# Issue order in the MLP of a decoder step: the second unit's first block, the last activations of a quarter, a third weight sum and the last unit's weight split are issued at other places

## The chip, the cores and the metric

The kernel runs on one NeuronCore of one Trainium2 chip. The metric is the time on the device in microseconds, the median of several runs. Engines: TensorE (PE), VectorE (DVE), ScalarE (ACT), GpSimd (POOL) and SyncE (SP), whose queue issues all the DMAs here.

## The reference, cut to what matters

One layer of a hybrid decoder for 512 prompt tokens and 64 sample tokens (8 requests of 8), width 1024. Attention, a gated recurrence and the first layer norm come first; the change lies in the MLP and the second layer norm behind it:

```python
x1 = _layer_norm(DN_ALPHA * x + g1 * mix, ln1_g, ln1_b, dtype)
u2 = x1 * (1 + sc2) + sh2
hid = jnp.square(jax.nn.relu(jnp.einsum('bsd,df->bsf', u2, w_up) + b_up))
ff = jnp.einsum('bsf,fd->bsd', hid, w_down) + b_down
x2 = _layer_norm(DN_ALPHA * x1 + g2 * ff, ln2_g, ln2_b, dtype)
```

`w_up` is 1024 x 4096, `w_down` 4096 x 1024, all in float32. To keep float32 accuracy at the matmul's fast format, every operand is split in a high part and a low part (the operand minus its high part), and a product is three matmuls: high by high, low of the data by high weight, high of the data by low weight.

## The kernel before, in words

**Weights.** A *unit* is a block of 1024 x 512 weights (eight k of 128 rows), loaded in two DMAs of 1 MB into `wraw` tiles; there are three such tiles (`NRAW`). `weights_done` frees one after its last reading and issues the next load. A weight block is split by an ACT copy to `whi` (the *cast*) and a subtraction to `wlo` (*low*), mostly on DVE. `split_k` (L362) does that for one k (128 x 512) into two tiles of the common pool `pages` (62 of them); the MLP's steps put theirs into the pool `parts` (6 tiles of 128 x 1024), which opens at L2092 in the memory that `front.close()` gives back.

**Order.** The order on each engine is the order in which the program issues; nothing is reordered afterwards, and an instruction whose input isn't there holds all behind it on its engine. A planner (`Engine`, `Side`) keeps a modelled clock of each engine, and between matmuls `side.pump` issues pieces of side work (layer norm, transposes, stores) whose modelled inputs are ready.

**The MLP.** `hid` is made and used in four quarters of 1024 columns. Tokens are handled in two halves of 288 columns (`HF`).

- *First unit of quarter 0* (L1796 to L1809): the first token half of its four blocks runs while the first layer norm's second half is still under way (`layer_norm_1(1)`, which makes the operands `U2_hi`, `U2_lo` tile by tile). Then `side.drain()`, then the second half of all four blocks, k by k into four PSUM banks (two of tag "lin", two of tag "att"), then `ups[n]`: for each bank ACT does relu, square and the high copy `hdh`, DVE the low part `hdl`.
- *The rest* is a list `seq` of 70 steps, run by the loop at L2101. `Plain` steps (L1884) are one block of 128 output columns over eight k, in two token halves (`pe(0)`, `pe(1)`, each 24 matmuls); they are the second unit of quarter 0 (steps 0 to 3) and the down-projections of quarters 0 to 2 (8 each). `Seventh` steps (L1944) are the seven products of Strassen's scheme for the up-projections of quarters 1 to 3: two units a quarter, seven steps f0 to f6 each, 24 matmuls a step. f1, f2, f4 and f5 need a sum of two weight blocks first (`sum`, on DVE, into `wraw`).
- In the loop, at step i, the order is: evacuation of step i-1's second half; cast of step i+1 if its `lag` is 1 (a Plain); low of step i+1; cast of step i+2 if its lag is over 2; if step i is a Plain right behind a Seventh: low part of step i-2's output (`sub`), activation of step i-1's (`fin`), its low part (`sub`); then `pe(0)` and its evacuation; on Sevenths the `fin` of i-1 and `sub` of i-2; the sum for step i+3 if its lag is over 2; sum and cast of step i+2 if its lag is 2; then `pe(1)`. f1 and f2 have lag 2, the other Sevenths lag 3.
- The first down-projection of quarters 1 and 2 uses `order`: second token half first, k in the order 0, 1, 2, 3, 6, 7, 4, 5, as k=4, 5 of that half (f5) and k=6, 7 of the first half (f6) come last.

**The end** (L2147 to L2283): the last quarter's down-projection in three units `ud[0]`, `ud[1]`, `ud[2]`. `blocks` makes output columns with the tokens 256 to 575 as the moving side, four blocks n a unit; behind each comes `gated` (DVE) and `tokens_major` (transposes, copies by ACT and DVE). `tiles` makes the tokens 0 to 255 as rows, two tiles c of 128 by 512 columns; `add_up` takes them into the residual on DVE, `moments` and `normalize` end a tile, DVE and POOL sharing the columns. The order is `blocks(ud[0])`, `blocks(ud[1])`, `tiles(ud[1])`, `tiles(ud[2])`. `ud[1]` is split in the last block of `blocks(ud[0])` (`pass_on`); `ud[2]` is split inside `tiles(ud[1])` at every second k: k 0 to 3 in tile 0 with the subtraction on POOL, k 4 to 7 in tile 1 with the subtraction on DVE. The side work normalises the tiles c = 2, 3, 4 in that same stretch.

Of the kernel before, what the change touches and what calls it, by code (L numbers as in the profile page):

```python
# [19 lines left out]
KT = D // 128  # L20
# [31 lines left out]
NPG = 62  # L52
NKV = 6
NWP = 6
AHEAD_K = 8
LN2 = 2500
SPH = 0
NRAW = 3
KV_AHEAD = 4
QB_AHEAD = 4  # L60
# [185 lines left out]
def decoder_step(ctx, tc, I, O):  # L246
# [24 lines left out]
    def bank(shape, tag, bufs=2):  # L271
        return psum.tile(shape, F32, name=tag, tag=tag, bufs=bufs)
# [86 lines left out]
        if j == len(u["blocks"]) - 1:  # L359
            weights_done(u["slots"])  # L360

    def split_k(u, k, eng=V):  # L362

        if k in u["w"]:
            return
        load_more(True)
        t = u["slots"][k // 4][2][:, k % 4]
        w = u["w"][k] = page([128, 512], "whi", F32R), page([128, 512], "wlo", F32R)
        A.activation(w[0], t, AF.Copy)
        eng.tensor_sub(w[1], t, w[0])  # L370
        if k % 4 == 3:
            weights_done(u["slots"][k // 4:k // 4 + 1])

# [1421 lines left out]

    u = mlp[0]  # L1796
    ups = [up_evac(0, n, True) for n in range(4)]
    for n in range(4):
        for m in range(n + 1, min(n + 3, 4)):
            split_once(u, m)  # L1800
        half(u, n, U2, 0, ups[n])
    side.drain()
    banks = [bank([128, HF], "lin" if n < 2 else "att") for n in range(4)]
    for k in range(KT):
        for n in range(4):
            mm_part(u["w"][n], 8, U2, 1, banks[n], (k,))
    for n in range(4):
        ups[n](1, banks[n])
        u["w"].pop(n)  # L1809

    def down_evac(qd, n):
        def evac(hf, ps):
            if qd == 0:
# [130 lines left out]
    class Seventh(Step):  # L1944


        def __init__(self, unit, f):
            self.U, self.f = unit, f
            self.lag = 2 if f in (1, 2) else 3

        def sum(self):
            f, b = self.f, self.U.blk
# [86 lines left out]
    for qd in range(4):  # L2039
        for n in range(8):  # L2040
            if qd == 0 and n < 4:
                continue
            if qd == 0:
                seq.append(Plain(mlp[1], n % 4, U2, up_evac(0, n)))
            elif n % 4 == 0:
                unit_ = Unit(mlp[qd * 4 + n // 4], qd, n)
                seq += [Seventh(unit_, f) for f in range(7)]
        if qd < 3:
            for n in range(8):

                order = {} if qd == 0 or n else {"order": ((1, (0, 1, 2, 3, 6, 7, 4, 5)), (0, range(KT)))}
                seq.append(Plain(mlp[qd * 4 + 2 + n // 4], n % 4, (Hd[0], Hd[1]), down_evac(qd, n), **order))
# [35 lines left out]
                yield 436, None  # L2088
        gate.append(True)

    front.close()
    parts["pool"] = ctx.enter_context(tc.tile_pool(name="parts", bufs=NWP))  # L2092
    n_down = len(seq) - 22

    def at(i, what, *a):
        if 0 <= i < len(seq):
            getattr(seq[i], what)(*a)

    at(0, "cast")
    at(0, "low")  # L2100
    for i, st in enumerate(seq):  # L2101
        if i < 4:
            for k in (2 * i, 2 * i + 1):
                for h in range(2):
                    G.tensor_mul(hv(hT[k], h), hv(hT[k], h), rstds[h])
        if i == 4:
            side.add("p", input_sums())
        if i == 12:
            side.drain()
        if n_down <= i < n_down + 8:  # L2110
            if i == n_down:
                side.flush(True)
                reload(0)
            if i < n_down + 7:
                reload(i - n_down + 1)
        at(i - 1, "ev", 1)
        if i + 1 < len(seq) and seq[i + 1].lag == 1:
            at(i + 1, "cast")
        at(i + 1, "low")
        if i + 2 < len(seq) and seq[i + 2].lag > 2:  # L2120
            at(i + 2, "cast")
        if i and isinstance(st, Plain) and isinstance(seq[i - 1], Seventh):
            for n in (1, 2):
                at(i - n, "fin" if n == 1 else "sub")
            at(i - 1, "sub")
        st.pe(0)
        st.ev(0)
        if not isinstance(st, Plain):
            at(i - 1, "fin")
            at(i - 2, "sub")  # L2130
        if i + 3 < len(seq) and seq[i + 3].lag > 2:
            at(i + 3, "sum")
        if i + 2 < len(seq) and seq[i + 2].lag == 2:
            at(i + 2, "sum")
            at(i + 2, "cast")

        for k in {5: (0, 1), 4: (2, 3), 2: (4, 5), 1: (6, 7)}.get(len(seq) - i, ()):
            split_k(ud[0], k)
        if i >= 6 and i % 2 == 0:
            copy_rows()  # L2140
        st.pe(1)
# [90 lines left out]
    def blocks(w, e):  # L2232
        for n in range(4):
            ps = bank([128, NT - NM], "lin")
            for k in range(KT):
                if n == 0 and k + AHEAD_K < KT:
                    split_k(w, k + AHEAD_K)
                for m, (xi, wi) in enumerate(TERMS):
                    PE.matmul(ps, w["w"][k][wi][:, n * 128:(n + 1) * 128], HD[xi][k][:, NM:NT],
                              start=(k == 0 and m == 0), stop=(k == KT - 1 and m == 2))  # L2240
# [5 lines left out]
            side.add("pr"[n % 2], tokens_major(4 * e + n))  # L2246
            side.pump(6 * 136.0)

    def pass_on(u, k, v):

        if k >= 2:
            u["w"].pop(k - 2)
        if k >= KT - AHEAD_K:
            split_k(v, k - KT + AHEAD_K)

    def tiles(w, e):
        for c in range(NM // 128):
            last = c == NM // 128 - 1

            def before(k):  # L2260
                if w is ud[1]:
                    if last and k >= 2:
                        w["w"].pop(k - 2)
                    if k % 2 == SPH:
                        split_k(ud[2], 4 * c + k // 2, V if c else G)

            for cols in (slice(0, 256), slice(256, 512)) if e and last else (slice(0, 512),):
                ps = mm_tokens(w["w"], HD, lambda t: t[:, c * 128:c * 128 + 128], range(KT), before, cols,
# [51 lines left out]
```

## Time and profile before

| | |
|---|---|
| median of 3 runs | 1382.89 us (1377.75 to 1384.52) |
| the profiled execution | 1378.02 us, its span 1376.2 us |
| mean granted TensorE clock | 0.989 |
| MLP and end | from 947 us (the first unit's first half) to the end |
| Strassen stretches | 1059 to 1105, 1160 to 1203, 1255 to 1300 us |
| `tiles` of the end | from 1336.8 us |

In timeline rows the columns are start, duration, engine, line, operation, output<-inputs, shape and count; in brackets the idle time of the engine before it and what ended it. All instructions carry L175, the line of the helper that issues them, so tiles tell them apart. Rows with a count (x4) are several instructions merged.

### The profile page before, as it was taken

To read this page: it belongs to the slowest core of one execution; us is meant where nothing else is said; L and a number is where in the kernel's file an instruction comes from. 1 tells how busy PE (TensorE), PEld (TensorE's weight loads), DVE (VectorE), ACT (ScalarE), POOL (GpSimd) and SP (SyncE) were. 2 spreads that over 40 slices of the span, in tenths; PEclk is the share of its full clock that TensorE was granted. 3 is DMA by queue.
4 is the path that set the end of the run, shared out by engine and by line. 5 is a ranking of instruction groups with operands and counts; after the bars stand their busy time and mean duration, and the time that the engine had idled before them with its cause. 6 is when DMAs were issued, how large, how long until landed. Compare 5 with 4: busy or idle time off the path is not lost.

```text
span 1376.2 us, 24394 instructions
## 1 busy us (share of the span) xinstructions
PE 1315.5 (96%) x9480; PEld 1209.6 (88%) x9480; DVE 840.3 (61%) x1674; ACT 519.9 (38%) x1161; POOL 324.7 (24%) x371
## 2 busy tenths in 40 slices
PE   6999999999999999999999999999899999999995
PEld 3889898899878887888989999998899999999994
DVE  2457556558767886666655436547455744756858
ACT  2423333332332222332232442325455732744732
POOL 1232023027417573234343300002410000000005
PEclk9999999999999999999999999999999999999998
DMA  9789899789988977776454313331054433544512
GB/s 306 246 309 323 270 299 355 242 273 324 281 290 286 317 252 242 231 252 200 138 167 141 100 62 123 130 123 62 0 177 153 169 138 117 206 161 154 215 61 69
DMA packets 186824, 274.11 MB, mean 199 GB/s; under 512 B 16012, under 2 KB 92628, under 8 KB 186196
## 3 DMA queue, kind: packets, MB, share of 16 engines
q1 hardware_dynamic: 186708, 272.54, 58.7%
q8 instruction: 75, 1.23, 0.4%
q14 instruction: 41, 0.34, 0.1%
HBM read 212.81 MB, written 76.46 MB: 210 GB/s over the span
## 4 chain that ended last, share of the span: by engine, by line
PE 76%; DVE 10%; DMA 5%; ACT 4%; issue 3%; POOL 1%; SPq 1%; DVEq 0%; POOLq 0%; ACTq 0%
PE lin L175 58%; PE att L175 9%; PE sx L175 6%; DVE wlo L175 4%; PE tr L175 3%; DMA wada<-in_w_ada_dram 2%; DVE res L175 1%; ACT whi L175 1%; ACT sn L175 1%; DMA qb<-qsc 1%; SPq L175 1%; ACT hdh L175 1%; DMA out_dram<-kv 1%; DVE Op L175 1%; DVE hf L175 1%
## 5 line engine op out<-in xcount | busy, mean ns | idle before, releaser
L175 DVE TENSOR_TENSOR wlo<-wraw,whi 128x512 fp32r<-128x512 f32 (+1 forms) x334 | 271.1, 849 | 122.9 <-ACT whi L175 120.0
L175 PE MATMUL lin<-uh,whi 128*128 128x288 f32 x992 | 298.7, 301 | 5.1 <-DVE hso L175 2.4
L175 PE MATMUL lin<-ul,whi 128*128 128x288 f32 x992 | 299.5, 302 | 1.2 <-DVE ul L175 1.2
L175 PE MATMUL lin<-uh,wlo 128*128 128x288 f32 x992 | 298.6, 301 | 1.9 <-DVE wlo L175 1.9
L175 ACT ACTIVATE whi<-wraw 128x512 fp32r<-128x512 f32 (+1 forms) x338 | 211.6, 676 | 118.6 <-PE lin L175 37.0
L175 PEld LDWEIGHTS lin<-ul,whi 128*128 128x128 f32 x992 | 188.0, 189 | 13.8 <-issue 11.0
L175 PEld LDWEIGHTS lin<-uh,whi 128*128 128x128 f32 x992 | 187.8, 189 | 11.3 <-issue 2.9
L175 PEld LDWEIGHTS lin<-uh,wlo 128*128 128x128 f32 x992 | 188.1, 190 | 6.6 <-issue 3.8
L175 POOL TENSOR_TENSOR qb<-qb,kv 128x512 f32<-128x512 f32 x96 | 128.5, 1355 | 203.5 <-PE att L175 65.1
L175 PE MATMUL lin<-hdl,whi 128*128 128x288 f32 (+1 forms) x448 | 133.5, 298 | 4.0 <-DVE hdl L175 4.0
L175 PE MATMUL lin<-hdh,whi 128*128 128x288 f32 (+1 forms) x448 | 134.1, 299 | 0.0
L175 PE MATMUL lin<-hdh,wlo 128*128 128x288 f32 (+1 forms) x448 | 133.2, 297 | 0.0
L175 PEld LDWEIGHTS lin<-hdl,whi 128*128 128x128 f32 x448 | 84.5, 189 | 4.7 <-DVE hdl L175 4.7
L175 POOL TENSOR_TENSOR wlo<-wraw,whi 128x512 fp32r<-128x512 f32 x4 | 6.4, 1603 | 331.5 <-ACT whi L175 331.5
L175 PEld LDWEIGHTS lin<-hdh,whi 128*128 128x128 f32 x448 | 84.5, 189 | 0.0
L175 PEld LDWEIGHTS lin<-hdh,wlo 128*128 128x128 f32 x448 | 84.4, 188 | 0.0
L175 PE MATMUL lin<-whi,uh 128*128 128x512 f32 x160 | 68.4, 428 | 1.3 <-ACT whi L175 1.1
L175 PE MATMUL lin<-wlo,uh 128*128 128x512 f32 x160 | 63.9, 400 | 1.9 <-DVE wlo L175 1.9
L175 DVE TENSOR_REDUCE sc<-qb 128x4 f32<-128x512 f32 x96 | 63.7, 678 | 2.6 <-POOL qb L175 2.4
L175 PE MATMUL lin<-whi,ul 128*128 128x512 f32 x160 | 63.1, 394 | 0.0
L175 PE MATMUL lin<-u2h,whi 128*128 128x288 f32 x176 | 53.0, 301 | 6.1 <-ACT whi L175 4.9
L175 POOL TENSOR_TENSOR hk<-hk,T 128x256 f32<-128x256 f32 (+1 forms) x48 | 40.2, 838 | 72.0 <-PE att L175 43.4
(421 smaller groups left out, 2884.5 us busy)
## 6 DMA issues: line engine op xcount, KB each, us to landing
wraw<-in_w_in_dram SPq DMA_DIRECT2D x42, 1024.0 KB
kv<-in_cache_kv_w_dram SPq DMA_DIRECT2D x144, 256.0 KB
qb<-qsc SPq DMA_DIRECT2D x96, 256.0 KB
wraw<-in_w_down_dram SPq DMA_DIRECT2D x18, 1024.0 KB
out_dram<-kv SPq DMA_DIRECT2D x64, 256.0 KB
wraw<-in_w_ada_dram SPq DMA_DIRECT2D x16, 1024.0 KB
wraw<-in_w_up_dram SPq DMA_DIRECT2D x16, 1024.0 KB
out_dram<-in_cache_kv_w_dram SPq DMA_DIRECT2D x32, 512.0 KB
```

What stands on the lines that cost most here:

```text
L175: return f(out, *args, **kw)
```

## The change

1. The second token half of the first unit is issued later in the program, behind `front.close()`, the opening of `parts` and cast and low of step 0, which so stand ahead of it.
2. In the first unit of each quarter (`n == 0`) f2 gets lag 3: its sum is issued one step earlier, and its cast at the beginning of step f0, ahead of that step's matmuls. The block for lag 2 is put ahead of the sum for lag 3, so that f1's sum still precedes f2's.
3. At a Plain behind a Seventh, `sub`, `fin`, `sub` of the two steps before are issued ahead of cast and low of the next step.
4. `ud[2]` is no longer split in `tiles(ud[1])`. In `blocks(ud[1])`, at k = 2 of block n, two k at a time are split by one ACT and one DVE instruction of 128 x 1024 into the `parts` pool (n = 0, 1, 2), and k = 6, 7 by `split_k` into pages (n = 3). POOL no longer subtracts weights. `AHEAD_K` was 8, which equals the number of k, so that taking it out changes nothing.

```diff
@@ split_k
-    def split_k(u, k, eng=V):
+    def split_k(u, k):
...
-        eng.tensor_sub(w[1], t, w[0])
+        V.tensor_sub(w[1], t, w[0])
@@ first unit (moved, see below)
-    for n in range(4):
-        for m in range(n + 1, min(n + 3, 4)):
-            split_once(u, m)
-        half(u, n, U2, 0, ups[n])
-    side.drain()
-    banks = [bank([128, HF], "lin" if n < 2 else "att") for n in range(4)]
-    for k in range(KT):
-        for n in range(4):
-            mm_part(u["w"][n], 8, U2, 1, banks[n], (k,))
-    for n in range(4):
-        ups[n](1, banks[n])
-        u["w"].pop(n)
@@ class Seventh
-        def __init__(self, unit, f):
+        def __init__(self, unit, f, after):
             self.U, self.f = unit, f
-            self.lag = 2 if f in (1, 2) else 3
+            self.lag = 2 if f == 1 or f == 2 and not after else 3
...
-                seq += [Seventh(unit_, f) for f in range(7)]
+                seq += [Seventh(unit_, f, n == 0) for f in range(7)]
@@ ahead of the loop
-    front.close()
-    parts["pool"] = ctx.enter_context(tc.tile_pool(name="parts", bufs=NWP))
...
+    for n in range(4):
+        for m in range(n + 1, min(n + 3, 4)):
+            split_once(u, m)
+        half(u, n, U2, 0, ups[n])
+    side.drain()
+    front.close()
+    parts["pool"] = ctx.enter_context(tc.tile_pool(name="parts", bufs=NWP))
     at(0, "cast")
     at(0, "low")
+    banks = [bank([128, HF], "lin" if n < 2 else "att") for n in range(4)]
+    for k in range(KT):
+        for n in range(4):
+            mm_part(u["w"][n], 8, U2, 1, banks[n], (k,))
+    for n in range(4):
+        ups[n](1, banks[n])
+        u["w"].pop(n)
@@ the loop
         at(i - 1, "ev", 1)
+        if i and isinstance(st, Plain) and isinstance(seq[i - 1], Seventh):
+            at(i - 2, "sub")
+            at(i - 1, "fin")
+            at(i - 1, "sub")
         if i + 1 < len(seq) and seq[i + 1].lag == 1:
             at(i + 1, "cast")
         at(i + 1, "low")
         if i + 2 < len(seq) and seq[i + 2].lag > 2:
             at(i + 2, "cast")
-        if i and isinstance(st, Plain) and isinstance(seq[i - 1], Seventh):
-            for n in (1, 2):
-                at(i - n, "fin" if n == 1 else "sub")
-            at(i - 1, "sub")
         st.pe(0)
         st.ev(0)
         if not isinstance(st, Plain):
             at(i - 1, "fin")
             at(i - 2, "sub")
-        if i + 3 < len(seq) and seq[i + 3].lag > 2:
-            at(i + 3, "sum")
         if i + 2 < len(seq) and seq[i + 2].lag == 2:
             at(i + 2, "sum")
             at(i + 2, "cast")
+        if i + 3 < len(seq) and seq[i + 3].lag > 2:
+            at(i + 3, "sum")
@@ blocks
-                if n == 0 and k + AHEAD_K < KT:
-                    split_k(w, k + AHEAD_K)
+                if w is ud[1] and k == 2:
+                    if n < 3:
+                        split_two(ud[2], 2 * n)
+                    else:
+                        split_k(ud[2], 6)
+                        split_k(ud[2], 7)
@@ new
+    def split_two(u, k):
+        load_more(True)
+        t = u["slots"][k // 4][2][:, k % 4:k % 4 + 2]
+        hi, lo = (wpart([128, 2, 512], nm) for nm in ("whi", "wlo"))
+        A.activation(hi, t, AF.Copy)
+        V.tensor_sub(lo, t, hi)
+        for i in range(2):
+            u["w"][k + i] = hi[:, i], lo[:, i]
+        if k % 4 == 2:
+            weights_done(u["slots"][k // 4:k // 4 + 1])
@@ tiles
             def before(k):
-                if w is ud[1]:
-                    if last and k >= 2:
-                        w["w"].pop(k - 2)
-                    if k % 2 == SPH:
-                        split_k(ud[2], 4 * c + k // 2, V if c else G)
+                if w is ud[1] and last and k >= 2:
+                    w["w"].pop(k - 2)
```

More of the change, by code (lines that the diff above doesn't have):

```diff
@@ L54 @@
 NWP = 6
-AHEAD_K = 8
 LN2 = 2500
-SPH = 0
 NRAW = 3
@@ L2252, in pass_on @@
             u["w"].pop(k - 2)
-        if k >= KT - AHEAD_K:
-            split_k(v, k - KT + AHEAD_K)
+        split_k(v, k)
     def tiles(w, e):
```

## Prediction

> **What bounds the kernel now.** I read the page first, then the waits of PE, then the timeline engine by engine at each of those waits.
>
> ```profile
> PE 1315.5 (96%) x9480; PEld 1209.6 (88%) x9480; DVE 840.3 (61%) x1674; ACT 519.9 (38%) x1161; POOL 324.7 (24%) x371
> ...
> ```
>
> ```profile
> PE lin L175 <- DVE wlo L175: 8.9, 9, 3.0
> PE lin L175 <- ACT whi L175: 6.0, 2, 4.9
> PE lin L175 <- DVE hdl L175: 4.0, 3, 1.6
> ...
> ```
>
> PE is busy for 96% of the span, so 60.7 us of idle PE is all that reordering can take out (slow matmuls aside). The change issues the same arithmetic in another order; it touches three of the sources: the split weights (`whi`, `wlo`) and the low part of the activations (`hdl`). What counts is therefore each wait by itself, and at the very end, where PE has run dry, the engine that sets the end.
>
> **Part 1, the second unit's first block.** The timelines of PE, of ACT (first row the last `u2h` of the layer norm), of DVE and of POOL around 975 us:
>
> ```profile
> 975.58 0.29 PE L175 MATMUL att<-u2h,wlo 128*128 128x288 f32 x1
> 980.75 0.40 PE L175 MATMUL lin<-u2h,whi 128*128 128x288 f32 x1 [4.88 <-ACT whi L175]
> 984.66 0.29 PE L175 MATMUL lin<-u2h,whi 128*128 128x288 f32 x1
> ```
>
> and, from the windows view of PE (stretch, length, busy time, count, granted clock, share and rate of the DMAs),
>
> ```profile
> 985.00:1060.00 75.00, 75.00 (x568) 1.00 0.42 151
> ```
>
> ```profile
> 969.80 1.10 ACT L175 ACTIVATE u2h<-u2t,b2m 128x288 fp32r<-128x288 f32 x2 [0.39 <-DVE u2t L175]
> ...
> 974.71 0.50 ACT L175 ACTIVATE rel<-lin,vT 128x288 f32<-128x288 f32 x1 [3.80 <-PE lin L175]
> ...
> 979.73 0.44 ACT L175 ACTIVATE hdh<-rel 128x288 fp32r<-128x288 f32 x1
> 980.08 2.18 ACT L175 ACTIVATE whi<-wraw 128x512 fp32r<-128x512 f32 x4
> 986.06 0.50 ACT L175 ACTIVATE rel<-lin,vT 128x288 f32<-128x288 f32 x1 [3.80 <-PE lin L175]
> ...
> 992.64 0.49 ACT L175 ACTIVATE rel<-lin,vT 128x288 f32<-128x288 f32 x1
> ...
> 999.39 0.48 ACT L175 ACTIVATE rel<-lin,vT 128x288 f32<-128x288 f32 x1
> ```
>
> ```profile
> 970.37 1.08 DVE L175 SCALAR_TENSOR_TENSOR u2l<-u2t,b2m,u2h 128x288 fp32r<-128x288 f32 x2
> ...
> 980.73 2.50 DVE L175 TENSOR_TENSOR wlo<-wraw,whi 128x512 fp32r<-128x512 f32 x4
> ```
>
> ```profile
> 987.26 3.33 POOL L175 TENSOR_TENSOR hT<-hT,lnr 128x288 f32<-128x288 f32 x4
> ```
>
> The columns are start, duration, engine, line, operation and tiles. The unit's second half ends with the matmul at 975.58, and the next starts at 980.75: ACT does twelve evacuation instructions from 974.71 to 980.2 first, and only then the cast that step 0 waits for. PE's pace undisturbed is 75.00 / 568 = 0.132 us a matmul, so 5.17 - 0.13 = 5.0 us are lost. Behind the wait PE is slow: from 980.75 to 984.66 there are 15 matmuls, 3.91 us where 15 x 0.132 = 1.98 would do, 1.9 us more (part 4 has the clock in such a stretch). The stall costs 6.9 us.
>
> With the cast ahead of the evacuations it runs behind the last `u2h`, from 970.9, and its subtraction behind the last `u2l`, from 971.5; a block's cast and low are half of the four merged instructions each, 1.1 and 1.3 us, so both are ready by 973 while PE works to 975.8. What they wait for is the load of that unit:
>
> ```profile
> GB/s 0 186 406 254 0 0 179 397 263 0 7 0 0 0 0 10 0 0 0 0 3 104 387 341 14 0 0 0 0 0 0 0 0 7 0 0 0 0 0 0
> ```
>
> These are 40 slices of 2.5 us from 900 us on; the weight traffic is over at 962.5, ahead of 970.9. What is late next is the bank: step 0 reuses the first "lin" bank, which ACT has read at 974.71 + 0.50 = 975.2, ahead of 975.7. So the 6.9 us go. Then step 1's cast stands behind the evacuations as before, to 981.2, and the read of step 0's first bank behind that, to 981.7; PE wants that bank at 975.7 + 48 x 0.132 = 982.0. From there ACT, which waits for POOL's square, which stands behind four products for the layer norm (the 3.33 us), gives a bank back every 992.64 - 986.06 = 6.6 and 999.39 - 992.64 = 6.75 us, where PE takes a step in 6.34. Before, the 5 us wait had given that chain a lead. Now the lead is 0.3 us and is gone after a step; two steps at 0.4 us each, so 0.8 us come back. Bounds: 0 and 1.6 (four steps at 0.4). **Gain 6.1 us** (5.3 to 6.9).
>
> **Part 2, the third sum.** DVE and the chain in the first unit of quarter 1, and PE in its second:
>
> ```profile
> 1062.33 1.22 DVE L175 TENSOR_TENSOR wlo<-wraw,whi 128x1024 fp32r<-128x1024 f32 x1 [2.40 <-ACT whi L175]
> ```
>
> ```profile
> 1065.57 3.20 PE sx L175 x24
> ```
>
> ```profile
> 1089.02 0.40 PE L175 MATMUL att<-t23h,wlo 128*128 128x288 f32 x1 [0.73 <-DVE wlo L175]
> ```
>
> f2's low part is ready at 1062.33 + 1.22 = 1063.5 and f2 starts at 1065.57: two microseconds to spare, and no wait of PE in that unit. The wait of 0.73 us for `wlo` is at f2 of the *second* unit of the quarter, whose lag stays 2. So this edit moves a DVE sum of 1.2 us (as long as a subtraction of that size) and a cast to an earlier place and takes no wait away. The DVE sum now stands behind f1's sum, which is the one that can wait for a load; it adds no wait of its own. **0 us**; bounds three times 1.2 us on either side, if an evacuation of the down-projection gets stuck behind it or f2 of the second unit profits; I see neither in the queue, and take 0.
>
> **Part 3, the last activations.** PE, ACT and DVE where quarter 1's down-projection begins, and PE in quarter 2:
>
> ```profile
> 1107.13 0.29 PE L175 MATMUL lin<-hdh,whi 128*128 128x288 f32 x1
> 1108.63 0.40 PE L175 MATMUL lin<-hdl,whi 128*128 128x288 f32 x1 [1.20 <-DVE hdl L175]
> ...
> 1206.74 0.40 PE L175 MATMUL lin<-hdl,whi 128*128 128x288 f32 x1 [1.21 <-DVE hdl L175]
> ```
>
> ```profile
> 1105.19 0.78 ACT L175 ACTIVATE hdh<-sn 128x288 fp32r<-128x288 f32 x2
> ```
>
> ```profile
> 1106.91 1.29 DVE L175 TENSOR_TENSOR wlo<-wraw,whi 128x512 fp32r<-128x512 f32 x2 [2.73 <-ACT whi L175]
> 1108.12 1.56 DVE L175 TENSOR_TENSOR hdl<-sn,hdh 128x288 fp32r<-128x288 f32 x4
> ```
>
> f5's high part is there at 1105.19 + 0.78 = 1106.0, but its low part is the first of the four merged instructions at 1108.12, because the next block's split stands ahead of it in DVE's queue and that waits for its cast. PE stands until 1108.63: 1.50 - 0.13 = 1.4 us, and the same in quarter 2 (1.21 of idle against 1.20). Issued first, the subtraction takes f5's part at 1106.0 and is done by 1106.8, ahead of 1107.26. f6's part is needed 42 matmuls (5.5 us) after the block begins, and the next block's cast, now behind `fin`, comes about 1 us later with a lead of a step. The third `hdl` wait of the list, 4.0 - 1.20 - 1.21 = 1.6 us, is that behind the loop's end, whose order stays. **Gain 2.8 us** (2.4 to 3.0).
>
> **Part 4, the last unit's weights.** PE's waits from 1310 us to the end, its clock behind the longest, its last matmul, and DVE's queue:
>
> ```profile
> PE lin L175 <- DVE wlo L175: 4.3, 3, 3.0
> ```
>
> ```profile
> 1360.10:1363.30 3.20, 3.20 (x16) 0.50 0.17 36
> ```
>
> ```profile
> 1366.58 0.28 PE L175 MATMUL att<-wlo,hdh 128*128 128x256 f32 x1
> ```
>
> ```profile
> 1322.87 0.48 DVE L175 SCALAR_TENSOR_TENSOR hT<-lin,mod,hT 128x256 f32<-128x256 f32 x1
> ...
> 1346.96 1.00 DVE L175 TENSOR_TENSOR wlo<-wraw,whi 128x512 fp32r<-128x512 f32 x1
> 1347.88 3.48 DVE L175 SCALAR_TENSOR_TENSOR res<-res,lnst,lgb 128x512 f32<-128x512 f32 x2
> 1351.29 3.46 DVE L175 TENSOR_TENSOR wlo<-wraw,whi 128x512 fp32r<-128x512 f32 x2
> 1354.67 3.43 DVE L175 SCALAR_TENSOR_TENSOR res<-res,lnst,lgb 64x512 f32<-64x512 f32 x2
> 1358.03 0.68 DVE L175 TENSOR_TENSOR wlo<-wraw,whi 128x512 fp32r<-128x512 f32 x1
> 1358.63 0.67 DVE L175 TENSOR_TENSOR gps<-lin,gate 128x512 f32<-128x512 f32 x1
> ...
> 1363.85 1.53 DVE L175 SCALAR_TENSOR_TENSOR res<-res,lnst,lgb 128x512 f32<-128x512 f32 x2
> ```
>
> ```profile
> 1326.10 0.55 PE L175 MATMUL tr<-ident,hT 128*128 128x128 f32 x3 [0.48 <-ACT res L175]
> ```
>
> PE loses 4.3 us here, and half of 3.2 us at a granted clock of 0.50. But the end is DVE's: from 1346.96 on, each row begins where the one before it ends, and the `gps` of a tile that PE has long finished comes at 1358.63. So the gain is what leaves DVE's queue. Between 1346.96 and 1358.63 four subtractions of weights stand between the normalisations; without them the next tile's `gps` starts after the two pairs, 1346.96 + 3.48 + 3.43 = 1353.9, which is 4.8 us earlier. A pair costs 1.53 us at 1363.85 and 3.4 where POOL works on its own share of the normalisation at the same time. Were all pairs at 1.53, DVE would be faster still, and PE would set the end: last matmul 1366.58 - 4.3 - 1.6 = 1360.7, 5.9 us earlier. I take 5.0, near the lower end, since POOL's share of the normalisations stays and only its four weight subtractions go. The Trainium skill (SBUF - State Buffer, section on SBUF's two separate sides) says that a DVE instruction with two SBUF inputs and a GpSimd instruction exclude each other, one being blocked for the other's whole length; by that rule the pairs stay slow and the gain is the 4.8, by the quick row it is the 5.9. The trace is on the rule's side, 3.4 against 1.53.
>
> What it costs in `blocks(ud[1])`: three DVE instructions of 128 x 1024 (1.22 us as the `wlo` at 1062.33) and two of 128 x 512 (0.68). DVE is late there as it is: the last gating of `ud[0]` starts at 1322.87, behind the splits of `ud[1]`, and PE has 0.48 us of wait at 1326.10 for a copy that hangs on this. The first wide subtraction lands in this backlog, so that this wait grows by up to 1.2 us; the later ones come where DVE has caught up. I take 1.2 (0 to 5, if every one is passed on to PE). **Gain 3.8 us** (0 to 5.9).
>
> **Sum.** 6.1 + 0 + 2.8 + 3.8 = 12.7 us. The profiled execution took 1378.02 us (span 1376.2), so 1365.3; the median of the three runs shown is 4.9 us above it, and from there it is 1370.2. The profiled run is about as fast as the fastest of the three (1377.75), so I put the forecast between the two, at 1367.8.
>
> **The rivals.**
>
> *The end profits in full.* If POOL, rid of the weights, is through early, the pairs run at their quick price and PE sets the end: 6.9 + 2.8 + 5.9 = 15.6, that is 1362.4 from the profiled run. Against it: two POOL instructions a tile and five tiles, by the code, remain in that stretch. Chance 0.12.
>
> *DVE's backlog takes the tail's gain.* Each split in `blocks(ud[1])` holds up gating and copies, and the transposes on PE wait: 3 x 1.22 + 2 x 0.68 = 5.0 us against the 5.0 of the tail. 6.1 + 2.8 = 8.9 is left: 1369.1 from the profiled run, 1374.0 from the median. For it speaks the wait at 1326.10, against it that PE has no further wait in those blocks. Chance 0.12.
>
> *The cast is first in the program and not in time.* Step 0's tile lies in a pool that opens over memory of closed ones; if a late reader of that memory holds it, part 1 gives nothing: 6.6 us, 1371.4 or 1376.3. Against it: the same tile is the first of that pool before. Chance 0.04.
>
> *Slower.* ACT's queue holds everything behind a cast whose load isn't there, the twelve evacuations now among them, and with the banks PE. If the unit's load landed later than 975.7 + 12.7 = 988.4, the whole gain would be gone; at 1000 the profiled 1378.0 would become 1378.0 - 12.7 + 24.3 = 1389.6. The traffic ends by 962.5, 26 us ahead of the point from which it decides. Chance 0.02.
>
> **How the numbers follow.** Forecast 0.70, and 0.12, 0.12, 0.04, 0.02 for the rivals. The range goes from below the full gain on the profiled run (1362.4) to above the backlog on the median (1374.0): 1360.5 to 1375. About 0.5%, 6.9 us, is what a measurement of this kernel can tell from no change, that is 1376.0: the first three cases lie below it and hold 0.94, of which I leave 0.02 to their upper edges; the void cast lies on it. So faster 0.92, same 0.06, slower 0.02.
>
> **What would show it.** Right: no wait for `whi` of 5 us behind the first unit, and no clock of 0.50 after it; waits of some tenths for a "lin" bank one to three steps later; no `hdl` wait at the first down-projection of quarters 1 and 2, but still one of 1.6 us ahead of the last units; `wlo` waits of 0.7 us at f2 of the second units as before; no POOL `wlo`; DVE unbroken from its third normalisation to the end, PE's last matmul well ahead of the last `gps`. Wrong: a new PE wait at `tr` or `lin` in `blocks(ud[1])` of over 2 us, or a tail in which the stretch from the first `tiles` matmul to the end shrinks by less than 3 us.

## The result, and the profile after

| | before | after |
|---|---|---|
| median | 1381.52 us (1377.75 to 1384.52, 4 runs) | 1363.84 us (1362.97 to 1364.36, 4 runs) |
| ratio to before | | 0.9875, interval 0.9846 to 0.9904 |
| profiled execution | 1378.02 us, span 1376.2 | 1364.36 us, span 1362.6 |
| PE idle in the span | 60.7 us | 1362.6 - 1307.2 = 55.4 us |

The change is faster, by 17.7 us between the medians and by 13.7 between the profiled executions. From the page of the changed kernel, the engines' busy time, and from its list of PE's waits, first for 985 to 1105 us, then from 1105 us to the end (total, times, longest):

```profile
PE 1307.2 (96%) x9480; PEld 1203.6 (88%) x9480; DVE 844.0 (62%) x1675; ACT 518.9 (38%) x1158; POOL 320.1 (23%) x367
```

```profile
PE att L173 <- DVE wlo L173: 0.7, 1, 0.7
```

```profile
PE lin L173 <- DVE hdl L173: 1.5, 1, 1.5
PE tr L173 <- ACT res L173: 1.2, 1, 1.2
PE sx L173 <- DVE wlo L173: 0.7, 1, 0.7
PE lin L173 <- DVE wlo L173: 0.7, 1, 0.7
```

The `whi` wait of 4.9 us is gone, two of the three `hdl` waits are gone, and so are the `wlo` waits of the end (4.3 us). What is left is the third `hdl` wait, three `wlo` waits of 0.7 us, and a `tr` wait that has grown from 0.5 to 1.2 us.

**Where to measure.** Both programs are the same up to the second half of the first layer norm, and still they do not reach it at the same time. The timelines of DVE, before and after, at the reciprocal that opens this half:

```profile
955.22 1.95 DVE L175 RECIPROCAL lnr<-lnr 128x288 f32<-128x288 f32 x1 [2.14 <-ACT lnr L175]
```

```profile
956.00 1.96 DVE L173 RECIPROCAL lnr<-lnr 128x288 f32<-128x288 f32 x1 [2.14 <-ACT lnr L173]
```

Among the 14 kernels profiled here, all alike up to that instruction, its start lies between 952.97 and 962.10 us. So I measure the change from there: 1376.2 - 955.22 = 420.98 us before, 1362.6 - 956.00 = 406.60 after, a gain of **14.4 us**. This lies inside the interval of the ratio (0.9904 and 0.9846 of 1381.52 are 13.3 and 21.3 us); the other 3.3 us of the medians' difference I put down to the front of the program, which the change does not touch; only the profiled executions show it by stretches.

The 14.4 us fall into five stretches, each between two PE or DVE instructions that can be found in every kernel: *a* from the end of the first unit's second half to the first matmul of the down-projection, *b* the Strassen steps of quarter 1, *c* the down stretch from the last Strassen matmul of a quarter to the first of the next, *d* the last units' `blocks` up to the first matmul of `tiles`, *e* from there to the end of DVE's last row, four merged instructions.

| kernel | a | b | c | d | e |
|---|---|---|---|---|---|
| before | 32.53 | 45.58 | 52.53 | 35.64 | 35.92 |
| after | 26.37 | 45.58 | 51.06 | 36.33 | 29.71 |
| p1_alone | 26.39 | 45.59 | 52.54 | 35.63 | 35.92 |
| p3_alone | 32.80 | 45.59 | 51.06 | 35.64 | 35.92 |
| p4_alone | 32.88 | 45.59 | 52.53 | 36.41 | 29.72 |
| no_p2 | 26.40 | 45.59 | 51.06 | 36.42 | 29.72 |
| lag3_both | 26.41 | 44.56 | 51.06 | 36.26 | 29.71 |
| act_square | 25.59 | 45.59 | 51.06 | 36.34 | 29.72 |
| early67 | 26.39 | 45.58 | 51.06 | 36.59 | 29.71 |
| all_dve | 26.41 | 45.59 | 51.06 | 36.44 | 29.44 |
| late_split | 26.37 | 45.58 | 51.06 | 35.72 | 29.71 |
| pool_more | 26.37 | 45.58 | 51.06 | 36.40 | 31.41 |
| combo | 25.83 | 44.54 | 51.05 | 36.25 | 29.70 |
| combined | 25.82 | 44.53 | 51.05 | 35.56 | 29.43 |

Stretch c occurs in quarters 1 and 2, so its 1.47 us count twice: 6.16 + 2.95 - 0.69 + 6.21 = 14.6, of which some tenths are given back between the stretches. Where nothing was changed a stretch repeats to 0.2 us, most to 0.02, except a (32.5 to 32.9) in the kernels that still have the long wait. That is what makes tenths readable here although the medians move by microseconds.

**Part 1 in the profile.** PE of the changed kernel where the second half ends and the two places where it pauses later, then ACT, then DVE:

```profile
976.35 0.29 PE L173 MATMUL att<-u2h,wlo 128*128 128x288 f32 x1
976.47 0.29 PE L173 MATMUL lin<-u2h,whi 128*128 128x288 f32 x1
...
995.97 0.40 PE L173 MATMUL lin<-u2h,whi 128*128 128x288 f32 x1
...
1002.72 0.40 PE L173 MATMUL lin<-hdh,whi 128*128 128x288 f32 x1
```

```profile
971.59 1.14 ACT L173 ACTIVATE whi<-wraw 128x512 fp32r<-128x512 f32 x2
...
988.67 0.48 ACT L173 ACTIVATE rel<-lin,vT 128x288 f32<-128x288 f32 x1
...
995.43 0.48 ACT L173 ACTIVATE rel<-lin,vT 128x288 f32<-128x288 f32 x1
...
1002.18 0.48 ACT L173 ACTIVATE rel<-lin,vT 128x288 f32<-128x288 f32 x1
```

```profile
972.24 1.29 DVE L173 TENSOR_TENSOR wlo<-wraw,whi 128x512 fp32r<-128x512 f32 x2
```

Cast and subtraction are done at 971.59 + 1.14 = 972.7 and 972.24 + 1.29 = 973.5, and step 0 starts at 976.47, 0.12 us behind the matmul before it. The read of a bank (`rel<-lin`) ends at 995.43 + 0.48 = 995.91 and 1002.18 + 0.48 = 1002.66, and PE goes on 0.06 us later both times: the bank chain that the prediction expected, every 995.43 - 988.67 = 6.76 us. Each of these two matmuls starts 0.42 us behind the one before it, where the pace is 0.13, and the one behind it 0.24 us later: 0.4 us are lost at each.

**Part 3 in the profile.** ACT and DVE of the changed kernel ahead of quarter 1's down-projection:

```profile
1099.90 0.78 ACT L173 ACTIVATE hdh<-sn 128x288 fp32r<-128x288 f32 x2
```

```profile
1100.38 0.83 DVE L173 TENSOR_TENSOR hdl<-sn,hdh 128x288 fp32r<-128x288 f32 x2 [1.50 <-ACT hdh L173]
```

The low part now starts 0.48 us behind the high part, and no subtraction of weights stands between them.

**Part 4 in the profile.** First two rows of the kernel before that the prediction did not show, DVE's first pair of normalisations and POOL's work beside it. Then of the kernel after DVE, POOL, PE's wait in `blocks(ud[1])` and its last matmul:

```profile
1342.10 2.45 DVE L175 SCALAR_TENSOR_TENSOR res<-res,lnst,lgb 128x512 f32<-128x512 f32 x2
```

```profile
1342.37 3.34 POOL L175 TENSOR_TENSOR wlo<-wraw,whi 128x512 fp32r<-128x512 f32 x2 [4.30 <-ACT whi L175]
```

```profile
1315.43 1.22 DVE L173 TENSOR_TENSOR wlo<-wraw,whi 128x1024 fp32r<-128x1024 f32 x1
...
1334.64 1.53 DVE L173 SCALAR_TENSOR_TENSOR res<-res,lnst,lgb 128x512 f32<-128x512 f32 x2
...
1338.58 6.09 DVE L173 SCALAR_TENSOR_TENSOR res<-res,lnst,lgb 128x512 f32<-128x512 f32 x4
1344.60 0.67 DVE L173 TENSOR_TENSOR gps<-lin,gate 128x512 f32<-128x512 f32 x1
1345.31 1.07 DVE L173 TENSOR_TENSOR res<-res,gps 128x512 f32<-128x512 f32 x1
...
1355.94 3.14 DVE L173 SCALAR_TENSOR_TENSOR res<-res,lnst,lgb 128x512 f32<-128x512 f32 x4
```

```profile
1335.77 10.05 POOL L173 TENSOR_TENSOR res<-res,lgb 128x512 f32<-128x512 f32 x6 [330.50 <-ACT res L173]
```

```profile
1318.65 0.55 PE L173 MATMUL tr<-ident,hT 128*128 128x128 f32 x3 [1.25 <-ACT res L173]
```

```profile
1351.77 0.28 PE L173 MATMUL att<-wlo,hdh 128*128 128x256 f32 x1
```

POOL has only the normalisation (`res`), DVE has no `wlo` behind 1334.64, and the `gps` of the next tile starts 1344.60 - 1338.58 = 6.0 us behind the statistics, where it took 1358.63 - 1346.96 = 11.7 before. The end is still DVE's: 1355.94 + 3.14 = 1359.08, 7.3 us behind PE's last matmul. PE's stretch at half clock is gone with the wait ahead of it, by the windows view (stretch, length, busy time, count, granted clock, share and rate of the DMAs):

```profile
1347.00:1351.70 4.70, 4.70 (x42) 1.00 0.14 31
```

### The profile page after: what moved, and what is told of

It reads as the page before. It is cut to its first block, busy times and chain, and to the rows that moved or that the text cites. A ratio compares the mean times of both kernels' runs of the same rounds, so it can differ in the third digit from the quotient of the medians.

```text
span 1362.6 us, 24388 instructions
## 1 busy us (share of the span) xinstructions
PE 1307.2 (96%) x9480; PEld 1203.6 (88%) x9480; DVE 844.0 (62%) x1675; ACT 518.9 (38%) x1158; POOL 320.1 (23%) x367
## 4 chain that ended last, share of the span: by engine, by line
PE 79%; DVE 9%; issue 4%; ACT 4%; DMA 2%; POOL 2%; SPq 1%; DVEq 0%; POOLq 0%; ACTq 0%
PE lin L173 59%; PE att L173 10%; PE sx L173 7%; PE tr L173 3%; DVE wlo L173 3%; DMA wada<-in_w_ada_dram 1%; DVE res L173 1%; ACT whi L173 1%; POOL hT L173 1%; ACT sn L173 1%; SPq L173 1%; DVE Op L173 1%; DVE sc L173 0%; DMA xtm<-in_x_prompt_dram 0%; DVE st L173 0%
## 5 line engine op out<-in xcount | busy, mean ns | idle before, releaser
L173 POOL TENSOR_TENSOR res<-res,lgb 128x512 f32<-128x512 f32 (+2 forms) x10 | 14.8, 1485 | 338.8 <-ACT res L173 338.4
L173 ACT ACTIVATE P<-P,stat_p 128x128 f32<-128x128 f32 (+1 forms) x48 | 20.0, 418 | 95.5 <-DVE stat_p L173 76.3
```

Source lines behind the costliest of these rows:

```text
L173: return f(out, *args, **kw)
```

## The experiments

The theory was the prediction's: each part acts by itself, at its own place, through the queue order of ACT or DVE. Against it stands that the parts could help or hinder one another, so that one carries most of the gain and the sum of the parts isn't the whole.

**One part at a time.** To the kernel before, the edits of one part only. The first has part 1:

```diff
@@ before, ahead of the loop
...
+    side.drain()
+    front.close()
+    parts["pool"] = ctx.enter_context(tc.tile_pool(name="parts", bufs=NWP))
     at(0, "cast")
     at(0, "low")
+    banks = [bank([128, HF], "lin" if n < 2 else "att") for n in range(4)]
...
```

> The kernel before with only the second unit's first block's cast and low ahead of the first unit's second half. My theory (the three gains lie in different stretches and add up): the quarter-1 Strassen steps start 6.1 us earlier counted from the last u2h copy, everything behind that keeps its distances, total about 6 us faster than before; the PE wait of 4.9 us for whi is gone, two waits of about 0.3 us for a bank one to three steps later. Rival (the gains share a cause, one stall handed from place to place): less than 4 us here, and a longer wait somewhere behind.

Part 3:

```diff
@@ before, the loop
+        if i and isinstance(st, Plain) and isinstance(seq[i - 1], Seventh):
+            at(i - 2, "sub")
+            at(i - 1, "fin")
+            at(i - 1, "sub")
         if i + 1 < len(seq) and seq[i + 1].lag == 1:
             at(i + 1, "cast")
         at(i + 1, "low")
...
-        if i and isinstance(st, Plain) and isinstance(seq[i - 1], Seventh):
...
```

> The kernel before with only sub, fin, sub ahead of the next step's cast and low at the first down-projection of quarters 1 and 2. My theory: two hdl waits of 1.2 us gone, 1.4 to 1.5 us per quarter, 2.9 us in all. Rival (the wait goes over to the next block's wlo): the same count of waits under another name, under 1 us.

Part 4:

```diff
@@ before, blocks
+                if w is ud[1] and k == 2:
+                    if n < 3:
+                        split_two(ud[2], 2 * n)
+                    else:
+                        split_k(ud[2], 6)
+                        split_k(ud[2], 7)
@@ tiles
-                    if k % 2 == SPH:
-                        split_k(ud[2], 4 * c + k // 2, V if c else G)
```

> The kernel before with only the last unit's weights split in the blocks ahead. My theory: from the first tiles matmul to the end 6.2 us less, the blocks ahead 0.8 us more (the wait for the transposes at n = 1 grows from 0.5 to 1.2 us), 5.4 us in all. Rival (the tail's gain hangs on the timing that the earlier parts set up): under 4 or over 7 us.

And the change without part 2:

```diff
-            self.lag = 2 if f == 1 or f == 2 and not after else 3
+            self.lag = 2 if f in (1, 2) else 3
```

> The changed kernel with f2 at lag 2 in all units, that is without the third sum issued earlier. My theory: as the changed kernel within 0.3 us of span; the three wlo waits of 0.73 us stand in the second units in both. Rival (the earlier sum takes DVE time out of the first unit and so helps): 1 to 3 us slower than the changed kernel, with a wlo wait in a first unit.

| kernel | median | ratio | from the reciprocal to the end | gain there |
|---|---|---|---|---|
| p1_alone | 1377.31 | 0.996 (0.9938 to 0.9981) | 1376.0 - 960.92 = 415.1 | 5.9 |
| p3_alone | 1378.09 | 0.9963 (0.9946 to 0.9979) | 1377.7 - 959.32 = 418.4 | 2.6 |
| p4_alone | 1373.30 | 0.9937 (0.9913 to 0.996) | 1370.4 - 954.46 = 415.9 | 5.0 |
| no_p2 | 1365.10 | 0.9871 (0.9844 to 0.9898) | 1366.8 - 960.09 = 406.7 | 14.3 |

Each part moves its own stretch by what it moves in the whole change, and no other stretch (a differs by 0.3 us in the two kernels that keep the long wait). The three gains add up to 13.5 of 14.4. So the parts add up, within 0.9 us, and 0.6 of these are the longer *a* of the two kernels. Part 2 is worth 0.1 us, nothing that can be told from none. In PE's waits of the last part alone, from 985 us on, the wait that it brings stands beside those that it leaves:

```profile
PE lin L175 <- DVE hdl L175: 4.0, 3, 1.6
PE tr L175 <- ACT res L175: 1.3, 1, 1.3
```

**Why part 2 does nothing.** By the trace f2's sum has room in a quarter's first unit, and the three `wlo` waits are at f2 of the second units, which the change leaves at lag 2. If so, the same edit there is worth what the waits cost.

```diff
-            self.lag = 2 if f == 1 or f == 2 and not after else 3
+            self.lag = 2 if f == 1 else 3
```

> The changed kernel with f2 at lag 3 in the second unit of each quarter as well. My theory (the 0.73 us wait at f2 of the second unit comes from its sum standing behind a low part in DVE's queue that waits for ACT): the three waits go, 0.8 us each, 2.5 us faster than the changed kernel. Rival (DVE and ACT are full in that stretch, 35 of 50 us each, so that the order does not matter): the waits go over to f3 or to hdl, within 0.5 us of the changed kernel.

PE's waits from 985 us on in this kernel:

```profile
PE lin L173 <- DVE hdl L173: 1.4, 1, 1.4
PE tr L173 <- ACT res L173: 1.3, 1, 1.3
```

All three `wlo` waits are gone; the Strassen stretches of the three quarters shrink by 1.02, 1.05 and 1.35 us, 3.4 together. That is more than 0.73 a wait, and the kernel after shows the rest around the wait: the matmul that waits, at 1083.73, starts 1.02 us behind the one before it, where the pace is 0.13, and its neighbours take 0.21 and 0.24, so 1.1 us are lost. In the third quarter two more matmuls of 0.25 and 0.24 follow one step later. So the change put its edit in the unit that had no wait. The median, 1363.49 us (ratio 0.9863, 0.9839 to 0.9887), is no clear step from the change's: 3.4 us are less than what the front of the program varies by.

**The bank chain of part 1.** ACT waits for POOL's square, and POOL for four products of the layer norm. With ACT doing the square in the four Plain steps, the chain is gone if that is its cause.

```diff
@@ the Plain steps of quarter 0
-                seq.append(Plain(mlp[1], n % 4, U2, up_evac(0, n)))
+                seq.append(Plain(mlp[1], n % 4, U2, up_evac(0, n, True)))
```

> The changed kernel with the squares of steps 0 to 3 on ACT instead of POOL. My theory (the banks of steps 1 to 4 come back late because ACT waits for POOL's square behind four products for the layer norm): the two gaps of PE of 0.4 us at the start of steps 3 and 4 go, 0.8 to 1 us faster than the changed kernel. Rival (ACT itself is the limit there, since 1.8 us of squares a step are added): the gaps stay or grow.

Stretch a falls by 0.78 us to 25.59: that is the chain's cost, and it is gone. But the whole gains nothing: from the reciprocal to the end of the second half this kernel takes 982.32 - 960.22 = 22.1 us, where every other takes 20.35 or 20.36. POOL of this kernel and of the kernel after, then DVE of both:

```profile
970.16 14.89 POOL L173 TENSOR_TENSOR hT<-hT,lnr 128x288 f32<-128x288 f32 x16
```

```profile
965.93 3.61 POOL L173 TENSOR_TENSOR hT<-hT,lnr 128x288 f32<-128x288 f32 x4
```

```profile
972.12 0.99 DVE L173 SCALAR_TENSOR_TENSOR u2t<-hT,g2m,lnr 128x224 f32<-128x224 f32 x1
973.03 0.82 DVE L173 TENSOR_TENSOR u2t<-u2t,b2m 128x64 f32<-128x64 f32 x1
973.78 1.06 DVE L173 SCALAR_TENSOR_TENSOR u2l<-u2t,b2m,u2h 128x288 fp32r<-128x288 f32 x1
```

```profile
969.98 0.44 DVE L173 SCALAR_TENSOR_TENSOR u2t<-hT,g2m,lnr 128x224 f32<-128x224 f32 x1
970.34 0.21 DVE L173 TENSOR_TENSOR u2t<-u2t,b2m 128x64 f32<-128x64 f32 x1
970.48 0.50 DVE L173 SCALAR_TENSOR_TENSOR u2l<-u2t,b2m,u2h 128x288 fp32r<-128x288 f32 x1
```

Without the squares in its queue POOL issues all 16 products in one piece, beside the last normalised operands on DVE: the three rows take 0.99, 0.82 and 1.06 us here, and 0.44, 0.21 and 0.50 where POOL is still, and PE needs these operands for the second half. That is 1.72 us more, against the 1.74 by which the stretch grew. So the squares, for which POOL waits, had kept its products out of DVE's way. The median is 1367.75 us, ratio 0.9876 (0.9848 to 0.9904).

**The third `hdl` wait.** It stands ahead of the last units, behind the loop's end. I took the splits of `ud[0]` ahead of it on DVE for its cause, and issued the last ones a step earlier.

```diff
-        for k in {5: (0, 1), 4: (2, 3), 2: (4, 5), 1: (6, 7)}.get(len(seq) - i, ()):
+        for k in {5: (0, 1), 4: (2, 3), 2: (4, 5, 6, 7)}.get(len(seq) - i, ()):
```

> The changed kernel with k = 6, 7 of the first down unit of the last quarter split one step earlier, together with k = 4, 5. My theory (the remaining hdl wait of 1.5 us ahead of the last units comes from these two subtractions standing ahead of hdl in DVE's queue): the wait falls to 0.5 us or less, 1 us faster than the changed kernel. Rival (f5's evacuation is held up by the subtractions that are now ahead of it, or the load isn't there yet): a wait of 1 us or more shows one step earlier, no gain.

The timeline of PE of this kernel where the wait had been:

```profile
1292.27 0.41 PE L173 MATMUL lin<-hdh,whi 128*128 128x320 f32 x1 [0.37 <-ACT hdh L173]
...
1294.18 0.41 PE L173 MATMUL lin<-hdh,whi 128*128 128x320 f32 x1 [0.42 <-ACT hdh L173]
```

The `hdl` wait of 1.5 us is gone, and two waits for `hdh`, ACT's activation, stand in its place: 0.37 and 0.42, each with two slow matmuls (0.41 to 0.42). Stretch d is 36.59 against 36.33, so nothing is gained. DVE and ACT of this kernel ahead of the first of the two waits:

```profile
1287.43 2.50 DVE L173 TENSOR_TENSOR wlo<-wraw,whi 128x512 fp32r<-128x512 f32 x4 [0.81 <-ACT whi L173]
```

```profile
1290.34 1.40 ACT L173 ACTIVATE sn<-sn 128x576 f32<-128x576 f32 x2 [0.98 <-DVE sn L173]
```

The two subtractions were the cause of the `hdl` wait, but their new place is no better. All four now stand in one piece ahead of an evacuation on DVE (`sn<-att,sn`), which starts 0.12 us ahead of the first down matmul, where in the kernel after it starts 1.41 us ahead. ACT waits 0.98 us for it, and its next `hdh` starts 1.80 us behind that matmul, where it was 0.51. So the rival had the mechanism: the evacuation is held up by the subtractions that are now ahead of it. Only the size of the new waits, 0.4 us each and not 1 us, was smaller than it said.

**POOL's share of the normalisation.** The tail term of the sum went wrong by 1.2 us, so I tested its price. If a DVE instruction and a POOL instruction exclude each other, DVE alone should take the whole normalisation of the tiles c = 2, 3, 4 in about the time that it takes with POOL's help.

```diff
@@ normalize
-                 [(0, 512, G), (512, 1024, V)])
+                 [(0, 512, G if c < 2 else V), (512, 1024, V)])
```

> The changed kernel with the tiles c = 2, 3, 4 normalised by DVE alone (four instructions a tile in place of two on DVE, one on ACT and two on POOL). My theory (a DVE instruction with two SBUF inputs and a POOL instruction exclude each other, so a pair takes 3.05 us beside POOL and 1.53 alone): four alone take 3.06 us, the end within 1 us of the changed kernel (the first pair, alone today, costs 1.5 more; the add behind gains 0.4). Rival (the two engines do work at the same time and 512-wide instructions are slow there for another reason): each tile 3 us longer, 7 to 9 us slower than the changed kernel.

DVE of this kernel:

```profile
1339.76 2.73 DVE L173 SCALAR_TENSOR_TENSOR res<-res,lnst,lgb 128x512 f32<-128x512 f32 x4
...
1343.13 0.69 DVE L173 TENSOR_TENSOR res<-res,gps 128x512 f32<-128x512 f32 x1
...
1344.53 5.36 DVE L173 SCALAR_TENSOR_TENSOR res<-res,lnst,lgb 128x512 f32<-128x512 f32 x8
```

Twelve instructions in 2.73 + 5.36 = 8.09 us, 0.67 each; in the kernel after it was six, the other half being POOL's, in 1.53 + 6.09 = 7.62. The 0.47 more come back in the residual sums, which cost 0.69 where they cost 1.07 beside POOL. Stretch e is 29.44 against 29.71: POOL's half of these columns saves nothing. The median is 1366.42 us (ratio 0.9872, 0.9846 to 0.9898). Now the other way, with POOL kept busy by results that nobody reads (three subtractions in tile 2, one in tile 3, added to the work of the change):

```diff
@@ normalize, POOL's branch
+        for _ in range({2: 3, 3: 1}.get(c, 0)):
+            G.tensor_sub(page([128, 512], "spare"), y, g)
         G.tensor_mul(y, y, g)
```

> The changed kernel with four more POOL subtractions of 128x512 (results unused) in the normalisations of tiles c = 2 (three) and c = 3 (one), as many as the change took from POOL there. My theory (my tail term was too small because it kept the durations of DVE's normalisations as they stood beside POOL's weight subtractions): DVE's normalisations and adds stand beside POOL for longer and take 1.5 to 1.75 us instead of 0.7 to 1.5, 1 to 2 us more from the first tiles matmul to DVE's last instruction (29.7 in the changed kernel). Rival (the term was too small for PE's sake, whose waits and slow clock went): less than 0.5 us more.

DVE of this kernel, then POOL:

```profile
1344.67 6.10 DVE L173 SCALAR_TENSOR_TENSOR res<-res,lnst,lgb 128x512 f32<-128x512 f32 x4
...
1353.88 1.67 DVE L173 TENSOR_TENSOR res<-res,gps 128x512 f32<-128x512 f32 x1
...
1357.19 0.89 DVE L173 SCALAR_TENSOR_TENSOR lnst<-lnst 128x1 f32<-128x1 f32 x1
```

```profile
1352.00 6.07 POOL L173 TENSOR_TENSOR res<-res,lgb 128x512 f32<-128x512 f32 x4
```

The tail grows by 31.41 - 29.71 = 1.70 us (one run, 1372.22 us), and two DVE rows carry it: the `res` sum of 1.67 us, 0.69 where POOL is still, and a small `lnst` of 0.89, 0.16 in DVE's timeline of the kernel after: 0.98 + 0.73 = 1.71. Both run beside POOL's normalisation, which the added work has pushed behind 1352. So POOL's work costs DVE time even though nobody waits for its result. The four normalisations in one row stay at 6.10: they had a POOL neighbour in the kernel after as well.

**The wait that part 4 brings.** The first wide split falls into DVE's backlog; issued at k = 6 instead of k = 2 of the first block, it should no longer hold up the copy.

```diff
-                if w is ud[1] and k == 2:
+                if w is ud[1] and k == (2 if n else 6):
```

> The changed kernel with the first pair of the last unit's weights split at k = 6 of block 0 instead of k = 2. My theory (the wait for the transposes in block 1 grew from 0.48 to 1.25 us because that first wide subtraction stands in DVE's backlog ahead of the gating and the copies): the wait falls back to about 0.5 us and the stretch from the last units' first matmul to the first tiles matmul from 36.3 to 35.6 us. Rival (any 1.2 us on DVE ahead of the copies costs the same, wherever it is put): the stretch stays at 36.3 or a wait shows a block later.

PE of this kernel at that copy:

```profile
1320.54 0.55 PE L173 MATMUL tr<-ident,hT 128*128 128x128 f32 x3 [0.55 <-ACT res L173]
```

The wait is back at 0.55 us, stretch d at 35.72, 0.6 less than after (one run, 1365.38 us).

**All that helped, together.** First lag 3 for every f2, with ACT's square in steps 1 to 3 only, so that POOL keeps one square ahead of its products:

```diff
-            self.lag = 2 if f == 1 or f == 2 and not after else 3
+            self.lag = 2 if f == 1 else 3
...
-                seq.append(Plain(mlp[1], n % 4, U2, up_evac(0, n)))
+                seq.append(Plain(mlp[1], n % 4, U2, up_evac(0, n, n > 4)))
```

> The changed kernel with f2 at lag 3 in every unit and the squares of steps 1 to 3 on ACT, those of step 0 left on POOL. My theory (the all-ACT version closed the gaps at steps 3 and 4 but let POOL run its sixteen products in one piece beside DVE's u2l and so lost 1.7 us ahead of it; with step 0's squares left on POOL the products stay behind them): the layer norm's reciprocal to the end of the second half 20.4 us as in the changed kernel, from there to the first down matmul 25.6 us instead of 26.4, and the Strassen stretches 44.5 us each. Rival (the products collide with DVE wherever they run): the 20.4 us stay, but the stretch behind is 26 us or more.

Stretch a is 25.83, and the stretch ahead of it is 977.29 - 956.94 = 20.35 again: with one square left to POOL its products keep out of DVE's way (one run, 1361.14 us). Then with the edits of `late_split` and `all_dve` as well:

> The changed kernel with all that paid: f2 at lag 3 in every unit, squares of steps 1 to 3 on ACT, the first pair of the last unit's weights at k = 6 of block 0, and tiles c = 2, 3, 4 normalised by DVE alone. My theory (the savings lie in separate stretches and add up): 3.4 + 0.5 + 0.6 + 0.3 = 4.8 us off the changed kernel, counted from the layer norm's reciprocal to the end, ratio to the kernel before about 0.984. Rival (DVE, which takes over POOL's share, is the bound from the blocks on, and late gating eats the 0.6): 3.5 us or less.

From 985 us on PE waits twice, 1.4 us for `hdl` and 0.6 us for the copy. From the reciprocal to the end it is 1356.3 - 954.88 = 401.4 us, 5.2 less than after. The median of five runs is 1360.65 us (1358.09 to 1363.04) against 1380.43 for the kernel before on the same chip, ratio 0.986 (0.9837 to 0.9883). That is the best of these kernels by its stretches; the intervals of the ratios of `after` and `combined` overlap, so the medians alone would not tell them apart.

## Why the prediction was right, point by point

- **Forecast and range.** 1367.8 was forecast, 1363.84 measured, inside 1360.5 to 1375.0 and faster by 1.25%. The sum, 12.7 us, stands against 14.4 us from the reciprocal on, so 1.7 of the 4.0 us between forecast and measurement are the sum's; the other 2.3 I put down to the front of the program, which varies by more than that from one execution to the next. No error of the sum made up for another: both sizes that were off, in part 4, put the forecast too high.
- **Part 1, 6.1 us: measured 6.06.** Stretch a shrank by 6.16, 0.1 comes back behind it. The stall, the slow clock and the 0.8 us that the bank chain gives back were all there at their sizes (`act_square` takes the chain away and finds 0.78). The two pauses stand three and four steps later, where the prediction said one to three. The load was in time.
- **Part 2, 0 us: measured none** (`no_p2`, 0.1). The reason was right too: the wait is in the unit that the edit leaves out (`lag3_both`, 3.4 us).
- **Part 3, 2.8 us: measured 2.95**, 1.47 a quarter, and the third `hdl` wait stayed.
- **Part 4, 3.8 us: measured 6.21 - 0.69 = 5.5.** This is the term that was mis-sized. For the backlog 1.2 was taken; the `tr` wait did grow by 0.77, and d by 0.69. For the tail 5.0 was taken, 6.2 measured. The step that failed is "I take 5.0, near the lower end, since POOL's share of the normalisations stays and only its four weight subtractions go". It left the pairs that stay near their old 3.48 and 3.43 and looked at no pair ahead of them. The first pair fell from 2.45 to 1.53 (0.92): before, two of POOL's weight subtractions ran beside it (from 1342.37 on), and in the changed kernel they are gone. The two other pairs took 3.48 + 3.43 before and 6.02 together after (0.9), and the residual sum behind them rose from 0.69 to 1.07 (-0.4) beside POOL's work. Against the 4.8 of the prediction's subtraction this gives 4.8 + 0.9 + 0.9 - 0.4 = 6.2. But the two other pairs did not get cheaper row by row. DVE's rows of the kernel after, the first of the four by itself and then the other three:

```profile
1338.58 0.99 DVE L173 SCALAR_TENSOR_TENSOR res<-res,lnst,lgb 128x512 f32<-128x512 f32 x1
```

```profile
1339.61 5.06 DVE L173 SCALAR_TENSOR_TENSOR res<-res,lnst,lgb 128x512 f32<-128x512 f32 x3
```

  The first takes 0.99 us, the others 1.66 to 1.77. Before, the first row of this chain was the `wlo` at 1346.96, with 1.00, the six behind it took 1.63 to 1.78 each, and the last `wlo`, with POOL through, 0.68. So a row beside POOL costs 1.7 us in both kernels, and the short first place went from a `wlo` to a normalisation: to take the merged rows of `wlo` off and leave the merged pairs as they were missed that. `pool_more` has the same four rows, 1.00 first and then 1.67 to 1.77. That POOL's work prices DVE's rows is shown in both directions (`all_dve`, `pool_more`).
- **The Trainium skill's rule.** The Trainium skill (SBUF — State Buffer, section SBUF: two separate sides) has a DVE instruction with two SBUF inputs and a GpSimd instruction exclude each other for a whole instruction. The runs agree: normalisations follow one another every 0.67 us alone and take up to 1.77 us beside POOL. Each of the four rows above ends 0.54 or 0.55 us behind the end of a POOL row that it started beside (POOL's end at 1339.03, 1340.73, 1342.43 and 1344.12 us), as if it had waited for that end. But the prediction used it on the normalisations alone; the weight subtractions that leave POOL are GpSimd instructions as well, and by the same rule they had a price on DVE.
- **The rivals.** "The end profits in full" came near in its sum (15.6 against 14.4) and not in its mechanism: PE's last matmul came 7.4 us earlier within the stretch (1366.58 - 1336.83 = 29.75 before, 1351.77 - 1329.37 = 22.40 after), but DVE sets the end as before; the prediction had put PE's gain there at 5.9. The measured median lies nearer to this rival's 1362.4 than to the forecast of 1367.8. The backlog took 0.7 of the 6.2. The cast was in time, nothing got slower.

What stays open: why the same program reaches the reciprocal at 953 in one execution and at 962 us in another. The traces show only where the 9.1 us lie: ahead of it PE is idle for 33.4 us in the earliest (`early67`) and 37.5 in the latest (`pool_more`), and its clock stands at 0.50 for 13.7 and 23.9 us.

## What to carry to other kernels

Measure a change from the last instruction that both kernels share, by stretches between instructions that every version has: here that turned medians which scatter by several microseconds into terms that repeat to a tenth. When work leaves one engine, price again the rows of the engine beside it, not only the queue that it leaves; and before giving work to POOL, see what the same instructions cost on DVE alone, since here POOL's half of a normalisation saved nothing. Before work is issued earlier to end a wait, see what stands behind its new place: the wait can go over to that (`early67`). And put the edit in the unit that has the wait (`lag3_both`).

## What the runs showed of the hardware

Before, PE's clock was granted at 0.50 for at least 3.20 us (from 1360.10 on) behind a wait of only 2.99 us, by the timeline of PE in the kernel before:

```profile
1358.76 0.49 PE L175 MATMUL lin<-wlo,hdh 128*128 128x512 f32 x1 [2.99 <-DVE wlo L175]
```

The Trainium skill (TensorE: Matmul & The Clock Gate, section Part 1: The HAM clock gate) puts the return to half clock behind an idle window of about 3.4 us; here a shorter wait did it. The length of the wait alone does not decide: in the kernel before, half clock also followed a wait of 1.85 us (from 452.54 us on), and in the kernel after none followed one of 3.21 us (from 505.14 us on).

An engine freed of a wait can do harm: POOL, no longer held up by ACT's evacuations, ran 16 products in 14.89 us beside DVE, and PE's next operands came 1.74 us later (`act_square`).
